# Two edits in a chunk-band attention layer: where background work may enter the VectorE queue, and which engine copies some of the queries

## The chip, the cores and the metric

The kernel runs on one core of one Trainium2 chip. The metric is the device time of one execution in microseconds (us), the median over several runs. The engines are named as in the profile: PE is TensorE's matmul unit and PEld its weight loads, DVE is VectorE, ACT is ScalarE, POOL is GpSimd, SP is SyncE, which here issues all DMAs.

## The reference, cut to what matters

Two layers of a streaming encoder are computed for a prompt of 2048 rows and a sample of 64 rows, each row 1024 wide. Layer A is a sliding-window attention with 16 heads and two key heads; layer B has 16 heads of its own keys and attends from each chunk of 64 rows to its own chunk and the eight before it.

```python
def gated_attention_layer(x_p, x_s, ck, cv, norm_g, w_in, q_g, k_g, w_out, ...):
    qp, kp, vp, gp = project(x_p, norm_g, w_in, q_g, k_g, n_heads, n_kv)
    op = prompt_band_attention(qp, kp, vp, past_chunks, bias_fn, sinks)
    y_p = x_p + (op * jax.nn.silu(gp)) @ w_out
    ...                                   # the same for the sample, with cached keys and values
def attend(q, k, v, bias, valid, sinks):
    s = jnp.einsum('bqkgd,bskd->bkgqs', qg, k).astype(jnp.float32) * (dh ** -0.5)
    s = s + bias.reshape(kv, g, tq, tk)
    ...
    p = jax.nn.softmax(s, axis=-1)        # layer B
```

`project` makes queries, keys, values and the gate with one matrix, and normalizes queries and keys per head.

## The kernel before, in words

**Precision by pairs.** Many operands are split in two numbers of fewer bits, a high part (ACT rounds it) and a low part (DVE takes the difference), and products are summed on PE over the parts. For the scores of layer B a head's high query `q1` stands twice in the 128 partitions, once in each half, and is multiplied with a key tile that holds the high keys in one half and the low keys in the other. So each query is needed in both halves. `q2` holds the low queries.

**The units.** The prompt is cut into eight units of 256 rows (0 to 7, each two tiles of 128), and the sample is unit 8 (`NU` is 8). The order in every pass is 0 to 6, the sample, then unit 7. Layer B makes eight passes, one for each pair of heads (`hp`). Each pass projects all nine units and attends in all nine; an entry of the list `its` is one unit of one pass.

**The order on PE** is written out by hand. `Filler` hands out the matmuls of the projections (L711 to L713) and of the output projections (L1858 to L1860) in small portions, and `pipeline` of layer B places the steps of attention between such portions. For each item it takes four steps (head and tile; the sample has one): `scores`, a share of background work, a portion of filler, then what is due from earlier steps (transposes of exponentials, products with the values). After the second step of a unit it calls `queries` for the next item; in the sample's only step it calls `queries` for unit 7 right after the sample's scores, and a portion of filler lies between that and unit 7's first scores.

**The order on the other engines** is made by a planner when the program is built, which places instructions by its own model of the times, within the dependencies. `Background` adds orderings to that: work put there (weight splits, norms, gates, low parts of queries) is released in portions by `bg.share`, and what is released is ordered behind the engine's "anchor", the last instruction given to `bg.anchor`. The ordering is no wait between engines.

**queries** (L1406) transposes the normalized queries and keys of an item into the one PSUM bank with the tag "tp"; ACT writes the high queries into one half of `q1` (L1431) and the high keys into half of `KA` or `KB` (L1432). For the sample the tiles are `QS`, `KSA` and `KSB`. `copies` then issues two DMAs that copy the high queries into the other half (L1436, shown as q<-q or QS<-QS); it is put into `held["later"]` and issued at the next `flush`. `low`, as urgent background work, makes the low queries (L1443) and low keys (L1447) on DVE. For the last two items of the whole layer (the sample and unit 7 of the last pass) `copies` isn't used, and `low` ends with an ACT copy instead (L1452). The last copy by DMA is kept in `held["copy"]`; the transposes by DMA of exponentials (L1553) are ordered behind it on SP's queue.

**scores** (L1459) computes one tile's scores into a bank with the tag "sb" (two buffers; L1492 and L1493, for the sample L1478). DVE adds the bias and takes the minimum of negated scores in one instruction (L1496; reading its accumulator is a second row of the profile). From the second pass on, except for the sample, DVE then adds a constant to the minimum (L1501, 128x1). ACT takes the exponential (L1505). The anchors are then the minimum `mi` on DVE and the exponential `ex` on ACT. After that `parts` makes the high part of the exponential on ACT (L1544) and the low part on POOL (L1545), and SP transposes both by DMA.

Other lines that will be named: L207 transposes two columns of maxima for the scales of the output weights, through the bank "tp"; L501 is the low part of a weight split; L807, L816 and L836 belong to the norms and the gate; L811 is POOL's power in the norm; L759 is ACT's evacuation of a projection's gate; L1650 is the product of transposed exponentials with the values.

## Time and profile before

| | |
|---|---|
| median of 3 runs | 2152.05 us |
| lowest, highest | 2145.67, 2154.64 us |
| the profiled execution | 2147.27 us, its span 2145.5 us |
| granted TensorE clock | 0.992 |
| busy: PE, DVE, ACT, POOL | 95%, 70%, 67%, 54% of the span |

The span goes from the first to the last instruction on the core. Layer B's attention runs from about 890 to 1990 us of it; one pass takes about 130 us. In the timeline an instruction's row has its start, its duration, engine, line, operation, output and inputs, and in brackets how long the engine stood idle before it and what ended that. A wait is put down to the releaser that came last by the profile.

### The profile page before, as it was taken

The numbers are of one execution on the slowest core, as the hardware profiler recorded it, in microseconds if no ns is written. First come the engines' busy times: TensorE is split into PE (matmuls) and PEld (weight loads), VectorE is DVE, ScalarE is ACT, GpSimd is POOL, SyncE is SP. The second block draws the span as 40 slices with busy tenths as digits, with TensorE's granted clock in tenths as the row PEclk, the third lists the DMA queues.
The fourth block names the chain that finished last, engine by engine and source line by source line (L and its number), as shares of the span: only waits on it lengthen the run. The fifth ranks groups of instructions, "written<-read, shape, count | busy, mean of one in ns | idle before, by whom it ended". The sixth has DMA issues, their size and how long they took to land.

```text
span 2145.5 us, 40906 instructions
## 1 busy us (share of the span) xinstructions
PE 2046.2 (95%) x12951; PEld 1467.4 (68%) x12951; DVE 1504.9 (70%) x4049; ACT 1428.7 (67%) x3610; POOL 1148.6 (54%) x1621
## 2 busy tenths in 40 slices
PE   7999999999999999888999999999999999898999
PEld 6887788778888999555555555555555555456887
DVE  6768778767767554677777777777867778577642
ACT  6878877767777333466667676777867768577420
POOL 5555544434445445774366676666766667566000
PEclk9999999999999999999999999999999999999999
DMA  8856545756544676744478799797887979668763
GB/s 277 269 168 209 176 155 191 211 168 212 163 149 133 211 220 182 243 149 156 136 173 205 186 194 224 169 229 177 194 213 175 241 156 202 153 144 193 228 198 116
DMA packets 512120, 404.96 MB, mean 189 GB/s; under 512 B 303696, under 2 KB 449376, under 8 KB 511872
## 3 DMA queue, kind: packets, MB, share of 16 engines
q1 hardware_dynamic: 511904, 402.35, 69.7%
q8 instruction: 102, 1.67, 0.3%
q14 instruction: 114, 0.93, 0.1%
HBM read 257.59 MB, written 73.43 MB: 154 GB/s over the span
## 4 chain that ended last, share of the span: by engine, by line
PE 62%; DVE 12%; ACT 8%; DMA 6%; issue 6%; POOL 4%; SPq 1%; ACTq 0%; DVEq 0%; POOLq 0%
PE pj L711 11%; PE pj L713 10%; PE pj L712 10%; PE pj L1858 4%; PE pj L1860 4%; PE pj L1859 4%; PE o L1650 3%; PE sa L900 2%; PE sb L1492 2%; PE tp L900 2%; PE sb L1493 2%; DVE p L1496 2%; DMA xraw<-in_x_rows_dram 1%; PE sa L1198 1%; DMA q<-q 1%
## 5 line engine op out<-in xcount | busy, mean ns | idle before, releaser
L711 PE MATMUL pj<-wh,xx 128*128 128x512 f16 (+2 forms) x1648 | 641.9, 389 | 5.3 <-ACT pb L734 2.9
L713 PE MATMUL pj<-wh,xx 128*128 128x512 f16 (+2 forms) x1648 | 623.9, 379 | 1.3 <-POOL xx L596 1.3
L712 PE MATMUL pj<-wh,xx 128*128 128x512 f16 x1024 | 390.1, 381 | 1.0 <-DVE wh L501 1.0
L1545 POOL TENSOR_TENSOR values<-p,values 128x640 f16<-128x640 f32 (+2 forms) x224 | 281.7, 1260 | 182.8 <-ACT values L1544 179.5
L1505 ACT ACTIVATE p<-p,nm 128x640 f32<-128x640 f32 (+5 forms) x264 | 199.6, 756 | 221.7 <-DVE nm L1501 175.1
L1858 PE MATMUL pj<-xx,wh 128*128 128x264 f32 (+1 forms) x1024 | 289.8, 283 | 5.8 <-DVE res L1868 3.1
L1859 PE MATMUL pj<-xx,wh 128*128 128x264 f32 (+1 forms) x1024 | 287.2, 280 | 0.0
L1496 DVE CUSTOM_DVE_ANT_0 p<-sb,BT 128x640 f32<-128x640 f32 (+5 forms) x272 | 196.5, 722 | 106.5 <-PE sb L1493 102.9
L712 PE MATMUL pj<-wl,xx 128*128 128x512 f32 (+1 forms) x624 | 233.8, 375 | 2.2 <-DVE wl L501 2.2
L596 POOL TENSOR_TENSOR xx<-xraw,xx 128x528 fp32r<-128x528 f32 (+4 forms) x144 | 185.4, 1307 | 89.3 <-ACT xx L595 75.9
L811 POOL TENSOR_TENSOR f<-f,mhalf 128x4 f32<-128x4 f32 (+2 forms) x187 | 191.5, 1025 | 11.4
L1312 POOL TENSOR_TENSOR o<-gt,o 128x256 f32<-128x256 f32 (+1 forms) x132 | 104.9, 795 | 152.7 <-ACT p L1215 91.7
L713 PEld LDWEIGHTS <-xx 128*128 128x128 f16 x1024 | 100.6, 98 | 125.4 <-issue 4.3
L816 DVE TENSOR_TENSOR pa<-pa,f 128x256 f32<-128x256 f32 (+3 forms) x221 | 143.9, 652 | 57.2 <-POOL f L811 52.4
L793 POOL TENSOR_TENSOR sq<-pa 128x256 f32<-128x256 f32 (+2 forms) x187 | 114.0, 610 | 120.1 <-ACT pa L747 79.2
L1215 ACT ACTIVATE p<-p,nm 128x257 f32<-128x257 f32 (+2 forms) x272 | 134.4, 497 | 50.5 <-DVE nm L1209 43.2
L711 PEld LDWEIGHTS <-xx 128*128 128x128 f16 x1024 | 100.9, 99 | 80.4 <-issue 2.2
L712 PEld LDWEIGHTS <-xx 128*128 128x128 f16 x1024 | 100.7, 98 | 80.1 <-issue 3.3
L1544 ACT CAST values<-p 128x640 f16<-128x640 f32 (+2 forms) x224 | 147.3, 658 | 8.3 <-DMA pt<-values 3.1
L1860 PE MATMUL pj<-xx,wl 128*128 128x264 f32 x512 | 145.4, 284 | 0.6 <-DVE wl L494 0.6
L1209 DVE CUSTOM_DVE_ANT_0 p<-sa,BT,nsink 128x256 f32<-128x256 f32 (+2 forms) x272 | 117.5, 468 | 38.3 <-PE sa L900 30.7
L1860 PE MATMUL pj<-xx,wh 128*128 128x264 f16 x512 | 141.3, 276 | 1.4 <-DVE wh L491 1.4
(279 smaller groups left out, 5023.4 us busy)
## 6 DMA issues: line engine op xcount, KB each, us to landing
xx<-xsb SPq DMA_DIRECT2D x112, 512.0 KB, 4.3
xx<-xsa SPq DMA_DIRECT2D x88, 512.0 KB, 4.9
xraw<-oga SPq DMA_DIRECT2D x64, 264.0 KB, 3.7
xraw<-ogb SPq DMA_DIRECT2D x64, 264.0 KB, 3.7
xsa<-xx SPq DMA_DIRECT2D x32, 512.0 KB, 4.0
wl<-in_w_in_b_dram SPq DMA_DIRECT2D x64, 256.0 KB, 5.1
wraw<-in_w_in_b_dram SPq DMA_DIRECT2D x56, 256.0 KB, 3.6
xraw<-in_x_dram SPq DMA_DIRECT2D x40, 256.0 KB, 3.9
```

The source lines that it names most:

```text
L596: nc.gpsimd.tensor_tensor(lo, rv, wide(hi), op=ALU.subtract)
L711: nc.tensor.matmul(ps[:n, :C], xh, wh, start=k == 0, stop=False)
L712: nc.tensor.matmul(ps[:n, :C], xh, wl, start=False, stop=False)
L713: nc.tensor.matmul(ps[:n, :C], xl, wh, start=False, stop=k == KC - 1)
L811: nc.gpsimd.tensor_tensor(fv, fv, mhalf[:n, :H], op=ALU.pow)
L1496: mi = nc.vector.tensor_tensor_reduce(out=p[r, :nk], in0=S[r, o : o + nk], in1=b, op0=ALU.add, op1=ALU.min, scale=1.0, scalar=3e38, accum_ ...
L1505: ex = nc.scalar.activation(p[:n, :nk], p[:n, :nk], AF.Exp, scale=-1.0, bias=it.nm[:n, c : c + 1], accum_out=it.sm[:n, c : c + 1],)
L1544: hi = nc.scalar.copy(two[:, :, 0, :], pv)
L1545: lo = nc.gpsimd.tensor_tensor(two[:, :, 1, :], pv, two[:, :, 0, :], op=ALU.subtract)
L1858: nc.tensor.matmul(ps[:, :OT], wh, oh, start=k == 0, stop=False)
L1859: nc.tensor.matmul(ps[:, :OT], wh, ol, start=False, stop=False)
L1860: nc.tensor.matmul(ps[:, :OT], wl, oh, start=False, stop=k == KC - 1)
```

## The change: an anchor behind the addition, and copies of queries by ScalarE

In `scores` the name `mi` is given to the addition (L1501) where there is one, so that `bg.anchor(mi, ex)` orders background work on DVE behind the addition and not only behind the minimum. In `queries` a test `direct` picks the sample and unit 7 of every pass (`it.unit[0] >= NU - 1`; the last two items are among them). For these ACT writes the high queries into the other half itself, in `queries`, straight from PSUM and next to the other activations; `copies` isn't put into `held["later"]`, so `held["copy"]` stays what it was. The ACT copy at the end of `low` is gone.

```diff
+        def direct(it):
+            return it.unit[0] >= NU - 1 or it in its[-2:]
+
         def queries(it):
...
             for hh, rows in enumerate(halves):
                 nc.scalar.activation(q1[hh][rows], qt[hh], AF.Identity, scale=gq[rows])
                 nc.scalar.activation(kd[hh][rows], kt[hh], AF.Identity, scale=gk[rows])
+                if direct(it):
+                    nc.scalar.activation(q1[hh][halves[1 - hh]], qt[hh], AF.Identity, scale=gq[rows])
 
             def copies():
                 for hh, rows in enumerate(halves):
                     held["copy"] = load(wide(q1[hh][halves[1 - hh]]), wide(q1[hh][rows])).ins
 
-            if it not in its[-2:]:
+            if not direct(it):
                 held["later"].append(copies)
 
             def low(hh, rows):
...
-                    if it in its[-2:]:
-                        nc.scalar.activation(
-                            q1[hh][halves[1 - hh]], qt[hh], AF.Identity, scale=gq[rows]
-                        )
                 return fn
...
             if turned(it, h):
-                nc.vector.tensor_scalar(
+                mi = nc.vector.tensor_scalar(
                     it.nm[:, c : c + 1], it.nm[:, c : c + 1], math.log(PB), 1.0,
                     op0=ALU.add, op1=ALU.mult,
                 )
```

## The prediction, made before the changed kernel was run

> **What bounds the kernel now.** I read the page first: its engine totals, the chain that ended last, and the costliest groups.

> ```profile
> span 2145.5 us, 40906 instructions
> PE 2046.2 (95%) x12951; PEld 1467.4 (68%) x12951; DVE 1504.9 (70%) x4049; ACT 1428.7 (67%) x3610; POOL 1148.6 (54%) x1621
> ...
> L1505 ACT ACTIVATE p<-p,nm 128x640 f32<-128x640 f32 (+5 forms) x264 | 199.6, 756 | 221.7 <-DVE nm L1501 175.1
> ```

> TensorE (PE) is busy for 95% of the span; VectorE (DVE) and ScalarE (ACT) for about 70%. So a microsecond is won only where PE stands still. The last row shows what edit one is about: ACT, ahead of the exponentials of layer B, stood idle for 175.1 us until the addition at L1501 had run. That is large, but it is ACT's idle time, not PE's. So I asked next for the waits of PE alone, in the stretch of layer B (1020 to 1975 us). Columns: who waited for whom, us in total, times, longest.

> ```profile
> PE sb L1492 <- DVE nm L1496: 11.5, 8, 1.9
> PE tp L207 <- DVE KB L1447: 6.9, 1, 6.9
> PE sb L1492 <- DMA q<-q: 6.1, 4, 1.9
> PE sb L1478 <- DMA QS<-QS: 4.8, 3, 1.8
> ...
> PE sb L1492 <- ACT q L1452: 1.5, 1, 1.5
> ...
> PE sb L1478 <- DVE nm L1501: 1.1, 1, 1.1
> ...
> PE sb L1492 <- ACT pb L759: 1.0, 1, 1.0
> ```

> No exponential appears as a releaser: PE doesn't wait for one directly. What the change can reach is the copies of the queries, q<-q and QS<-QS, 10.9 us. The last two rows belong to them as well, as will be seen; L1452 is in the pair of items where ACT makes the copy already.

> The timeline of one head pair shows the place; the other pairs repeat it. Columns: start, duration, engine and line, and in brackets the engine's idle time before it with its releaser. First all engines:

> ```profile
> 1296.07 0.28 DVE L1443 SCALAR_TENSOR_TENSOR QS<-tp,qsc,QS 64x64 fp32r<-64x64 f32 x1 [1.30 <-ACT KSB L1432]
> ...
> 1297.00 1.40 SPq L1436 DMA_DIRECT2D QS<-QS  x2
> ...
> 1300.99 0.83 ACT L1505 ACTIVATE p<-p,nm 128x640 f32<-128x640 f32 x1 [1.57 <-DVE nm L1501]
> ...
> 1301.17 0.53 PE L1478 MATMUL sb<-KSA,QS 128*128 128x320 f32 x2 [1.30 <-DMA QS<-QS]
> ...
> 1301.94 0.72 ACT L1544 CAST values<-p 128x640 f16<-128x640 f32 x1
> ...
> 1305.25 0.45 ACT L1431 ACTIVATE q<-tp,qf 64x256 f16<-64x256 f32 x1
> ...
> 1306.46 0.46 ACT L1432 ACTIVATE KB<-tp,kf 64x256 f16<-64x256 f32 x1
> ...
> 1306.80 1.13 SPq L1436 DMA_DIRECT2D q<-q  x2
> ...
> 1306.95 0.47 DVE L1443 SCALAR_TENSOR_TENSOR q<-tp,qf,q 64x256 f16<-64x256 f32 x1 [0.75 <-ACT KB L1432]
> ...
> 1307.46 0.48 DVE L1447 SCALAR_TENSOR_TENSOR KA<-tp,kf,KA 64x256 f16<-64x256 f32 x1
> ...
> 1310.62 0.32 PE L1492 MATMUL sb<-KA,q 128*128 128x384 f16 x1 [1.71 <-DMA q<-q]
> ```

> Then DVE alone, around the sample's scores:

> ```profile
> 1298.63 0.81 DVE L1496 CUSTOM_DVE_ANT_0 p<-sb,BT 128x640 f32<-128x640 f32 x1
> 1299.37 0.08 DVE L1496 DVE_READ_ACCUMULATOR2_ANT nm<- 128x1 f32 x1
> 1299.37 0.41 DVE L807 TENSOR_REDUCE f<-sq 128x4 f32<-128x256 f32 x1
> 1299.70 1.13 DVE L836 SCALAR_TENSOR_TENSOR pb<-sq,pb 128x128 f32<-128x128 f32 x1
> 1300.75 0.14 DVE L1501 TENSOR_SCALAR nm<-nm 128x1 f32<-128x1 f32 x1
> 1302.01 0.42 DVE L816 TENSOR_TENSOR pa<-pa,f 128x256 f32<-128x256 f32 x1 [1.11 <-POOL f L811]
> 1302.35 0.48 DVE L1496 CUSTOM_DVE_ANT_0 p<-sb,BT 64x320 f32<-64x320 f32 x1
> ```

> PE reaches the sample's scores (L1478) at 1301.17 - 1.30 = 1299.87 and is held by the copy of QS. It reaches the first score of unit 7, which follows, at 1310.62 - 1.71 = 1308.91, with everything ready but the copy of q. Two stalls in a pass, 3.0 us.

> **Edit two, the copies by ACT: what goes.** By the order of units, "sample or unit 7" are two of nine items of each head pair. Seven pairs lose two DMAs in each; the eighth makes its copies on ACT already, and there they move ahead of the low parts. The stalls that the copies own: at unit 7, 6.1 us and the 1.0 put down to L759 (an evacuation that only stands last in the record; the stall has the place and size of its sisters), together 7.1 in five passes; at the sample, 4.8 and the 1.1 put down to L1501 (the same reason), together 5.9 in four.

> **What comes.** The added instruction exists in the trace, in the last pair:

> ```profile
> L1452 ACT ACTIVATE QS<-tp,qsc x2: 307/309/311, 1960.7 to 1962.2; 64x64 fp32r<-64x64 f32 x2
> L1452 ACT ACTIVATE q<-tp,qf x2: 467/469/471, 1970.7 to 1972.2; 64x256 f16<-64x256 f32 x2
> ```

> 14 x 0.31 + 14 x 0.47 = 10.9 us of ACT, which is idle a third of the time. They aren't free, though: DVE's low parts (L1443, L1447) began at 1306.95, when the last of the four activations (1306.46 + 0.46) had ended, though the first was done at 1305.70; at the sample the row of 1296.07 says the same, behind KSB. I take it that they will wait for all six. Four activations took 1305.25 to 1306.92, 0.42 each; two more put the low parts of unit 7 back by 0.84. PE needs the first pair of low parts only, as another pass shows, where PE started while the second L1443 was running:

> ```profile
> 1179.42 0.49 DVE L1443 SCALAR_TENSOR_TENSOR q<-tp,qf,q 64x256 f16<-64x256 f32 x1
> ...
> 1179.50 0.32 PE L1492 MATMUL sb<-KA,q 128*128 128x384 f16 x1 [0.95 <-DMA q<-q]
> ```

> So what is late next at unit 7 is L1447 of KA: 1307.46 + 0.48 + 0.84 = 1308.78, just under PE's arrival at 1308.91, and the stall would be gone. But PE will arrive earlier, by what the sample's stall gave back (1.3), while ACT's queries hang on the sample's minima (1302.35), and these stand behind L816, which waited for GpSimd and not for PE. If these stay where they are, 1.2 us of each stall returns. Between 0 and 1.2 I take 0.5: with S ready earlier the minima may well be placed ahead of L816. Unit 7 gives 7.1 - 5 x 0.5 = 4.6.

> At the sample the next late thing is the bank of scores, free when the minimum of 1298.63 ends (1299.37 + 0.08 = 1299.45), or up to 0.6 later if the two small activations push DVE's low parts and with them that minimum: at most 1300.07, against 1299.87. I take 0.1 each: 5.9 - 0.4 = 5.5.

> In the last pair L1492 waited for the first L1452, 1.5 us; the low parts, pushed by the copies now ahead of them, take its place. I keep 0.4 of it.

> One cost stands against this. The second-longest row of the waits, L207, is a transpose for which the one bank "tp" must be free of unit 7's queries, between pairs 6 and 7:

> ```profile
> 1830.28 0.49 DVE L1447 SCALAR_TENSOR_TENSOR KB<-tp,kf,KB 64x256 f16<-64x256 f32 x1
> ...
> 1830.92 0.58 PE L207 MATMUL tp<-ident,top 128*1 128x128 f32 x2 [6.88 <-DVE KB L1447]
> ```

> There all four low parts count, and 0.84 more is paid in full: +0.8.

> The transposes by DMA (L1553) on SP's queue are ordered behind the last copy; that copy is now unit 6's, so around the sample they may go out earlier, and 28 issues fewer stand before them. Nobody waits for their result: their reader L1650 idled 0.9 us in all, for something else.

> ```profile
> L1650 PE MATMUL o<-pt,values 128*128 128x256 f16 (+1 forms) x1176 | 125.7, 255 | 0.9 <-ACT o L1622 0.9
> ```

> So that is 0.

> [...]

> **Edit one, the anchor on the addition.** The same DVE work in another order: L836 (1.13 us above) behind L1501, not ahead. The exponential of 1300.99 could start at 1299.7. The cost on DVE is nothing, since the addition runs anyway; work moved behind it is 0.14 later. What it gains is ACT's time, and PE waits for ACT hardly anywhere. The longest row of PE's waits, 11.5 us for minima at L1496, has its regular place at unit 6:

> ```profile
> 1280.03 1.30 DVE L501 SCALAR_TENSOR_TENSOR wh<-wl,gsb,wh 128x512 f16<-128x512 f32 x1
> ...
> 1281.56 0.48 DVE L1443 SCALAR_TENSOR_TENSOR q<-tp,qf,q 64x256 f16<-64x256 f32 x1
> ...
> 1283.77 0.81 DVE L1496 CUSTOM_DVE_ANT_0 p<-sb,BT 128x640 f32<-128x640 f32 x1
> ...
> 1284.65 0.32 PE L1492 MATMUL sb<-KA,q 128*128 128x384 f16 x1 [1.36 <-DVE nm L1496]
> ```

> DVE has there 1.30 us of L501, then the low parts of the next unit's queries, four of 0.48 or so by their rows at unit 7, and only then the minimum that PE waits for; the addition's place among them changes nothing in their sum. So I take 0, between -11.5 (all of that row) and the loss of the third rival.

> **Sum.** -4.6 - 5.5 - 0.4 + 0.8 = -9.7, say -10. The profiled execution took 2147.27 us (span 2145.5), 4.8 under the median of the runs, 2152.05, whose spread is 9; so 2137 for an execution like the profiled one and 2142 for the median. About 0.5% (10.7 us) is what a measurement of this kernel can tell from no change, so the forecast lies on that edge.

> **Rivals.**
> *More is won (0.15).* Earlier exponentials bring the casts, GpSimd's work and the evacuations forward, DVE gets through unit 6 earlier, and some of the 11.5 us goes too, besides all of unit 7. For it: ACT's 175.1 us of idling. Against: DVE full at that place. At most 7.1 + 5.9 + 1.5 + 11.5 = 26; with half of the 11.5 it is 20, less the 0.8: 2133.
> *The wait only changes its name (0.18).* Unit 7 keeps 1.2 in each of five passes (7.1 - 6.0 = 1.1 won), the sample waits 0.2 in each of four (5.1 won): 1.1 + 5.1 - 0.8 = 5.4, 2147. For it: L816 waiting for GpSimd, and low parts that begin only behind the whole batch. Against: the sample's scores come earlier.
> *Slower (0.14).* On ACT an exponential that is ready earlier gets a place ahead of the next unit's queries (L1431). With the cast behind it that is 0.83 + 0.72 = 1.55 us, by which low parts, the next minimum and the bank come later; where DVE is full, as at unit 6, PE pays it all. It decides from seven such places on (10 / 1.55); at two of nine units in each of seven passes it costs 14 x 1.55 = 21.7: 2142 + 21.7 = 2164. For it: the order on ACT is made anew by a planner. Against: the queries are asked for before the scores whose exponential would pass them, and most units have slack, since PE's wait for minima has only 8 entries.

> **How the numbers follow.** The forecast has 0.53, within 2138 to 2147 (the stalls of unit 7 gone wholly and the sample's as well, 7.1 + 5.9 + 1.5 = 14.5 less 0.8; or the second rival's 5.4 as its other end). The range goes from 2127 (the first rival nearly whole) to 2155 (the second, with the spread of the runs, and the mild part of the third). Faster by over 0.5%: the first rival and under half of the forecast, 0.15 + 0.25 = 0.40. Slower by over 0.5%: most of the third, 0.12. The rest, 0.48, is within.

> **What would show it.** Right: no QS<-QS among PE's waits, and no q<-q at unit 7; L1478 with under 0.3 us of idle time; at unit 7 a rest of 0 to 1.2 with DVE (KA, L1447) as the releaser; L207 near 7.7; ACT's wait for L1501 well under 175, with PE's wait for L1496 still near 11. Wrong: L1492 waiting for L1496 in more than 15 places, or the stall at unit 6 gone.

## The result, and the profile after

Six executions of each kernel: 2163.87 us after (2160.74 to 2166.85) against 2148.55 before, a ratio of 1.0068 [1.0048, 1.0088]. The change costs 0.7%; the forecast was 0.5% less, with 2155 as its upper end. The profiled execution took 2165.26 us, its span was 2163.4, its mean granted TensorE clock 0.986 (before 0.992).

The page after:

```profile
PE 2060.8 (95%) x12951; PEld 1472.0 (68%) x12951; DVE 1515.9 (70%) x4049; ACT 1441.9 (67%) x3638; POOL 1140.8 (53%) x1621
```

PE runs the same 12951 matmuls and is busy 14.6 us longer. From here on lines of `queries` and `scores` are numbered as in the changed kernel: the minimum is L1497, the addition L1502, the exponential L1506, the copy by ACT L1437, the low queries and keys L1448 and L1452, POOL's low part L1546, the sample's product on POOL L1616. PE's waits of layer B (1020 to 1990 us):

```profile
PE sb L1493 <- DVE nm L1497: 14.7, 7, 2.7
PE o L900 <- POOL o L1616: 11.6, 6, 3.0
PE tp L207 <- DVE KB L1452: 5.6, 1, 5.6
PE pj L711 <- DVE values L754: 4.8, 5, 1.0
PE o L1651 <- DVE o L1311: 3.8, 7, 0.9
PE sb L1493 <- DVE f L807: 2.6, 1, 2.6
```

The waits for the copies (QS<-QS, and q<-q but for 0.5 us) are gone, as the second edit means them to be. In their place stand three others: the second row was 3.2 us before and is now 11.6; the fourth and the fifth were under 1 us each. The first has grown by 3.2, and the 2.6 us put down to L807 are one more stall at its regular place, unit 6.

Where the time goes is read by passes. I took the five passes between the sample's scores of the second pair and of the seventh. These are the last lines of two tables by windows, before first, then after; the first number is the length:

```profile
sum 650.70, PE 627.08 PEld 360.59 DVE 489.96 ACT 480.46 POOL 439.11; mean PE 125.42 PEld 72.12 DVE 97.99 ACT 96.09 POOL 87.82
```

```profile
sum 672.00, PE 638.84 PEld 363.99 DVE 505.12 ACT 491.00 POOL 436.37; mean PE 127.77 PEld 72.80 DVE 101.02 ACT 98.20 POOL 87.27
```

The five passes are 21.3 us longer: PE stands still 33.2 us instead of 23.6 (+9.5), and is busy 11.8 us longer with the same work. (The span grew by less, 17.9, because the changed kernel came to the first of these passes 3.8 us earlier.) Two stalls come back in every pass: in these five, PE's stalls at unit 6 come to 13.3 us instead of 6.7, and those behind the sample to 11.3 instead of 3.3. One is at unit 6, where VectorE's order has changed. DVE before and then after, start and duration first:

```profile
1409.07 0.82 DVE L1496 CUSTOM_DVE_ANT_0 p<-sb,BT 128x640 f32<-128x640 f32 x1
...
1409.81 0.68 DVE L175 TENSOR_REDUCE most<-wraw 128x1 f32<-128x512 f32 x1
1410.41 1.30 DVE L501 SCALAR_TENSOR_TENSOR wh<-wl,gsb,wh 128x512 f16<-128x512 f32 x1
...
1411.76 0.14 DVE L1501 TENSOR_SCALAR nm<-nm 128x1 f32<-128x1 f32 x1
...
1414.16 0.81 DVE L1496 CUSTOM_DVE_ANT_0 p<-sb,BT 128x640 f32<-128x640 f32 x1
```

```profile
1415.93 0.82 DVE L1497 CUSTOM_DVE_ANT_0 p<-sb,BT 128x640 f32<-128x640 f32 x1
...
1417.15 1.42 DVE L501 SCALAR_TENSOR_TENSOR wh<-wl,gsb,wh 128x512 f16<-128x512 f32 x1 [0.40 <-ACT wh L498]
1418.49 0.14 DVE L1502 TENSOR_SCALAR nm<-nm 128x1 f32<-128x1 f32 x1
1418.56 0.67 DVE L175 TENSOR_REDUCE most<-wraw 128x1 f32<-128x512 f32 x1
...
1419.28 0.47 DVE L1448 SCALAR_TENSOR_TENSOR q<-tp,qf,q 64x256 f16<-64x256 f32 x1
...
1421.49 0.81 DVE L1497 CUSTOM_DVE_ANT_0 p<-sb,BT 128x640 f32<-128x640 f32 x1
```

Before, the maximum L175 (0.68) ran in the time between the minimum and the weight split L501. Now L175 may only come behind the addition, L501 still stands ahead of it, and DVE idles 0.40 us for ACT. But ACT isn't what holds L501 longest. POOL has a low part in work there, before and then after:

```profile
1409.76 1.40 POOL L1545 TENSOR_TENSOR values<-p,values 128x640 f16<-128x640 f32 x1
```

```profile
1416.62 1.40 POOL L1546 TENSOR_TENSOR values<-p,values 128x640 f16<-128x640 f32 x1
1424.52 0.73 DVE L501 SCALAR_TENSOR_TENSOR wh<-wl,gsb,wh 128x512 f16<-128x512 f32 x1
```

L501 takes 0.73 us in its shortest rows, in which no low part runs beside it (last row). Here it takes 1.30 and 1.42, and both times it ends 0.55 us behind the low part and 2.64 us behind the start of the minimum. So in either order DVE came past L501 only behind POOL's low part. L175 used to lie in that time, and now it comes on top. In three of the other four passes the idle time is only 0.12 us and L501 takes 1.70 instead, and the sum is the same: from minimum to minimum DVE needs 5.56 us instead of 5.09.

That is 0.47 of the 1.30 us by which the stall grows here. The rest is a later beginning: PE reaches the bank 4.59 us after the first of these minima started before the change, and 3.77 us after it now. PE's side of it before:

```profile
1415.03 0.32 PE L1492 MATMUL sb<-KA,q 128*128 128x384 f16 x1 [1.37 <-DVE nm L1496]
```

And after:

```profile
1419.32 0.38 PE L713 MATMUL pj<-wh,xx 128*128 128x512 f16 x1
1422.37 0.32 PE L1493 MATMUL sb<-KA,q 128*128 128x384 f16 x1 [2.67 <-DVE nm L1497]
...
1423.32 0.63 PE L712 MATMUL pj<-wh,xx 128*128 128x512 f16 x1
1423.75 0.63 PE L713 MATMUL pj<-wh,xx 128*128 128x512 f16 x1
...
1426.31 0.39 PE L713 MATMUL pj<-wh,xx 128*128 128x512 f16 x1
```

Behind the stall the matmuls of 512 columns start 0.43 us apart, eight times, until they fall back to 0.21: the stall has cost the clock as well, about 1.7 us more. In a row of a table by windows the third number from the end is the granted clock, here 0.50:

```profile
1422.90:1426.31 3.41, 3.41 (x11) 1.20 (x9) 3.30 (x7) 2.76 (x8) 2.31 (x3) 0.50 0.96 289
```

The trace's records of the granted clock have seven such stretches of 3.41 us in the five passes, five at the stalls of unit 6 and two behind the sample's, and none before the change. Half of 7 x 3.41 is 11.9 us: that is PE's longer busy time.

The other stall is behind the sample, on POOL's queue. Before, then after:

```profile
1459.52 0.32 POOL L1615 TENSOR_TENSOR o<-G,o 128x64 f32<-128x64 f32 x1 [0.98 <-DVE o L1614]
...
1461.33 1.40 POOL L1545 TENSOR_TENSOR values<-p,values 128x640 f16<-128x640 f32 x1
```

```profile
1465.12 0.46 DVE L1615 TENSOR_TENSOR o<-tp,o 64x64 f32<-64x64 f32 x2
1466.49 0.14 POOL L348 MEMSET BT<- 64x64 f32 x1 [1.75 <-DMA BT<-skew]
1466.59 1.39 POOL L1546 TENSOR_TENSOR values<-p,values 128x640 f16<-128x640 f32 x1
1467.94 0.31 POOL L1616 TENSOR_TENSOR o<-G,o 128x64 f32<-128x64 f32 x1
```

The low part of an exponential, 1.4 us long, now stands ahead of the sample's small product. PE's transpose L900 waits for that product: 1.93 us in this pass, up to 2.96 in others, against at most 0.7 before.

The low part isn't all of it. The product's operands were ready at 1465.58, when L1615 ended. Until 1466.49 POOL stood still: ahead of the low part, a fill of the bias tile (L348) waited for the load of that tile. Before the change the fill stood ahead of the product too, but its load was there in time. On SP's queue that load went out between two transposes of exponentials, and now it goes out behind both, before and then after:

```profile
1455.42 0.33 SPq L347 DMA_DIRECT2D BT<-skew  x1
1456.62 1.27 SPq L1553 DMA_TRANSPOSE pt<-values  x1
```

```profile
1459.03 4.53 SPq L1554 DMA_TRANSPOSE pt<-values  x2
1463.66 0.62 SPq L347 DMA_DIRECT2D BT<-skew  x1
```

So of the 2.36 us by which the product is late, 0.91 are the load's and 1.45 those of the fill and the low part. In each of the five passes the fill waits like this, 1.75 to 2.25 us in all.

### The profile page after: what moved, and what is told of

The parts are those of the page before. It is cut to its first block, busy times and chain, and to the rows that moved or that the text cites. A ratio compares the mean times of both kernels' runs of the same rounds, so it can differ in the third digit from the quotient of the medians.

```text
span 2163.4 us, 40853 instructions
## 1 busy us (share of the span) xinstructions
PE 2060.8 (95%) x12951; PEld 1472.0 (68%) x12951; DVE 1515.9 (70%) x4049; ACT 1441.9 (67%) x3638; POOL 1140.8 (53%) x1621
## 4 chain that ended last, share of the span: by engine, by line
PE 62%; DVE 12%; ACT 8%; issue 6%; DMA 6%; POOL 5%; SPq 1%; ACTq 0%; POOLq 0%; DVEq 0%
PE pj L711 11%; PE pj L712 11%; PE pj L713 11%; PE pj L1859 4%; PE pj L1861 4%; PE pj L1860 4%; PE o L1651 3%; PE sa L900 2%; DVE p L1497 2%; PE tp L900 2%; DVE wh L501 2%; PE sb L1493 2%; PE sb L1494 2%; PE sa L1198 1%; POOL f L811 1%
## 5 line engine op out<-in xcount | busy, mean ns | idle before, releaser
L1546 POOL TENSOR_TENSOR values<-p,values 128x640 f16<-128x640 f32 (+2 forms) x224 | 282.2, 1260 | 144.8 <-ACT values L1545 133.3
L1506 ACT ACTIVATE p<-p,nm 128x640 f32<-128x640 f32 (+5 forms) x264 | 199.5, 756 | 219.0 <-DVE nm L1502 165.4
L1497 DVE CUSTOM_DVE_ANT_0 p<-sb,BT 128x640 f32<-128x640 f32 (+5 forms) x272 | 196.6, 723 | 122.7 <-PE sb L1494 119.4
L811 POOL TENSOR_TENSOR f<-f,mhalf 128x4 f32<-128x4 f32 (+2 forms) x187 | 188.8, 1011 | 11.6
L816 DVE TENSOR_TENSOR pa<-pa,f 128x256 f32<-128x256 f32 (+3 forms) x221 | 146.8, 666 | 60.3 <-POOL f L811 56.8
L712 PEld LDWEIGHTS <-xx 128*128 128x128 f16 x1024 | 101.6, 99 | 86.8 <-issue 11.2
```

The source lines that it names most:

```text
L712: nc.tensor.matmul(ps[:n, :C], xh, wl, start=False, stop=False)
L811: nc.gpsimd.tensor_tensor(fv, fv, mhalf[:n, :H], op=ALU.pow)
L1497: mi = nc.vector.tensor_tensor_reduce(out=p[r, :nk], in0=S[r, o : o + nk], in1=b, op0=ALU.add, op1=ALU.min, scale=1.0, scalar=3e38, accum_ ...
L1506: ex = nc.scalar.activation(p[:n, :nk], p[:n, :nk], AF.Exp, scale=-1.0, bias=it.nm[:n, c : c + 1], accum_out=it.sm[:n, c : c + 1],)
L1546: lo = nc.gpsimd.tensor_tensor(two[:, :, 1, :], pv, two[:, :, 0, :], op=ALU.subtract)
```

## The experiments

Ratios are to the kernel before, run on the same chip beside them, with the 95% interval.

### Which of the two edits?

`anchor_only` takes the first edit alone (its lines are numbered as before the change), `copies_only` the second; `copies_sample` and `copies_unit7` take the second for one of its two items:

```diff
# copies_sample                                  # copies_unit7
-            return it.unit[0] >= NU - 1 or it in its[-2:]
+            return it.unit[0] == NU or it in its[-2:]      # or: == NU - 1
```

> Edit one alone: the anchor on the addition; all copies of queries stay as before. Theory H (the changed kernel is late because PE, relieved of the copies, runs into work of DVE, ACT and POOL that it cannot hurry, and its clock falls behind the longer stalls): the copies still hold PE, so nothing much changes: ratio 0.998 to 1.002, the stall at unit 6 stays 1.2 to 1.6 us, clock 0.992. Rival O (the new order of background work is itself the loss: weight splits behind the addition lengthen DVE's way to the minimum that frees the bank): ratio 1.005 to 1.010, the stall at unit 6 grows to 2 us or more and the clock falls to 0.988 or lower.

> Edit two alone: ACT copies the queries of the sample and of unit 7 in every pass; the anchor stays on the minimum. Theory H: the stalls at the sample and at unit 7 are gone, the one at unit 6 grows to over 2 us with the clock falling behind it, ratio 1.003 to 1.008. Rival O: the stalls go and little comes in their place, ratio 0.993 to 0.997.

> Half of edit two: ACT copies the queries of the sample only; unit 7 of every pass but the last keeps its copy by DMA; the anchor stays on the minimum. Theory H: the stall of the sample (1.3 to 1.8 us in four passes) moves to unit 7, where the copy's issue hangs on ACT and not on PE: 1.7 becomes 2.5 to 3; ratio 0.999 to 1.003. Rival O: 5 us won, ratio 0.997.

> The other half of edit two: ACT copies the queries of unit 7 only; the sample keeps its copy by DMA; the anchor stays on the minimum. Theory H: the stall of unit 7 (1.0 to 1.9 us in five passes) goes, and half of it or more comes back at unit 6 of the next pass; ratio 0.998 to 1.004. Rival O: 6 us won, ratio 0.997.

Measured: `anchor_only` 1.0116 [1.0101, 1.0131], `copies_only` 0.9972 [0.996, 0.9985], `copies_sample` 1.0017 [1.0004, 1.0031], `copies_unit7` 0.9992 [0.9978, 1.0006]. My first theory, that the copies take the cover from PE and run it into the other engines' chain, falls: the copies win 6.0 us. The order of the background work loses 25 us by itself, and has both stalls; the one behind the sample has grown more:

```profile
PE sb L1492 <- DVE nm L1496: 16.2, 8, 2.7
PE o L900 <- POOL o L1615: 13.9, 6, 3.5
```

In `copies_only` PE waits 4.9 us for the evacuation L754 and 4.6 for the low query L1448, both at unit 7. In `copies_sample`:

```profile
PE sb L1493 <- DMA q<-q: 18.4, 7, 3.7
```

With the copy by ACT at the sample alone, the stall saved there comes back at unit 7, whose DMA copy PE now awaits for 18.4 us instead of 6.1. The two copies only pay together.

### Which operation is in the wrong place?

Four variants of the whole change. `scan_behind_min` puts L175 back behind the minimum, `product_on_dve` takes the sample's product off POOL's queue, past the fill and the low part, `both_back` does both, and `stall_filled` fills the stall behind the sample with matmuls:

```diff
# scan_behind_min: bg.first holds the minimum, bg.anchors the addition
-            if r.ins.engine in bg.anchors:
-                behind(r.ins, bg.anchors[r.ins.engine])
+            if r.ins.engine in bg.first:
+                behind(r.ins, bg.first[r.ins.engine])
# product_on_dve
-            nc.gpsimd.tensor_tensor(o, it.G[:, 0:HD], o, op=ALU.mult)
+            nc.vector.tensor_tensor(o, it.G[:, 0:HD], o, op=ALU.mult)
# stall_filled
             tp = o_bank()
+            for _ in range(6):
+                nc.tensor.matmul(tp[:, 0:512], held["VH"][:, 0, 0], KA[:, 0:512], start=True, stop=True)
             transpose(tp[0:HD, 0:P], it.o)
```

> The changed kernel with one thing put back: the maximum over a weight tile (L175) is again ordered behind the minimum, not behind the addition; all other background work stays behind the addition. Theory M (two places carry the loss: at unit 6 VectorE idles 0.40 us ahead of the low part L501 because L175 no longer fills that gap, which makes PE's stall 1.4 -> 2.7 us and lowers the clock behind it; at the sample GpSimd takes the next low part ahead of the sample's product, 0.65 -> 2.3 us): the stall at unit 6 goes back to at most 1.7 us a pass, the slow matmuls behind it (near 1287, 1423, 1557, 1691, 1824) go, and the time falls by about 8 us to a ratio near 1.003. The stalls for L1616 stay (total near 11) unless the later exponential moves them too. Rival P (DVE's chain is full: whichever work is placed where, the stall only moves): the sum of PE's waits for DVE stays within 2 us of that of the changed kernel and the ratio stays 1.005 to 1.009.

> The changed kernel with the sample's product (L1616, 128x64) on VectorE instead of GpSimd, so that no low part and no fill of the bias tile stands ahead of it. Theory M: PE's wait for L1616 (11.6 us in six places) falls below 2 us, the slow matmuls behind those of over 2.2 us go, and the time falls by about 10 us, to a ratio of 1.000 to 1.003; the stall at unit 6 stays at 14.7 us in all. Rival P: the wait returns as one for VectorE in the same place (over 1 us each), ratio 1.005 to 1.009.

> Both of these in the changed kernel: L175 behind the minimum, the sample's product on VectorE. Theory M: both losses go, the clock is back at 0.991 or more, and the time is near that of the copies alone or a little better: ratio 0.993 to 0.999. Rival P: above 1.003.

> The changed kernel with six matmuls of 512 columns (1.3 us at full clock) into the sample's free bank ahead of the transpose that waits for L1616; what they write is written over. They lie in time in which PE idles where the stall is over 1.3 us, and keep it from idling long. If the long stalls themselves lower the clock behind them (theory C): no slow matmuls behind the sample's stalls (near 1199, 1335, 1962), so 1 to 2 us less behind each of three, against up to 1 us more where the stall is shorter: ratio 1.003 to 1.007, clock up by 0.001 to 0.002. If the clock is lowered by something else (rival D): the slow matmuls stay, the clock as in the changed kernel (0.986), and the time is the same or up to 4 us longer, ratio 1.006 to 1.010.

Measured: 1.0034 [1.0017, 1.0051], 1.0025 [1.001, 1.004], 1.0046 [1.0027, 1.0065] and 1.0085 [1.0064, 1.0107]. Each of the first two gives back about half, as theory M has it, but the two don't add. PE's waits say why; `scan_behind_min`, `product_on_dve`, `both_back`:

```profile
PE o L1651 <- DVE o L1311: 7.9, 8, 1.2
...
PE o L900 <- POOL o L1616: 0.3, 1, 0.3
```

```profile
PE sb L1493 <- DVE nm L1497: 16.2, 8, 2.7
```

```profile
PE o L1651 <- DVE o L1311: 7.9, 8, 1.2
...
PE o L900 <- DVE nm L1502: 3.4, 4, 0.8
```

With L175 behind the minimum DVE needs 4.97 us from minimum to minimum at unit 6, and the stall there is 1.6 us in three of the five passes. In the planner's new order POOL's low part and the fill stand behind the sample's product again: 11.6 us become 0.3. So nothing is left for the second repair to win; it adds a wait for DVE of 3.4 us. In place of the two stalls a third has grown, for the sums of outputs L1311, which are ordered behind the addition as well.

In `stall_filled` no slow matmuls follow the stalls behind the sample (in the changed kernel they do after the two of 2.25 and 2.96 us in these passes), but the six matmuls take 1.3 us of PE each time, and the time doesn't fall. By its time this run decides nothing between C and D; that the stretches of 0.50 behind the sample's stalls are gone speaks for C, and so do the counts at the end.

### Work that meets POOL's low part

In the groups of DVE's instructions (1170 to 1820 us) three kinds have a longer mean after the change, L816, L836 (473 to 512 ns) and L501 (1159 to 1218 ns). With L175 back L816 is at 840. L816 before, then after:

```profile
L816 DVE TENSOR_TENSOR pa<-pa,f 128x256 f32<-128x256 f32 (+1 forms) x85 | 59.4, 700 | 28.0 <-POOL f L811 27.0
```

```profile
L816 DVE TENSOR_TENSOR pa<-pa,f 128x256 f32<-128x256 f32 (+1 forms) x83 | 62.1, 753 | 32.6 <-POOL f L811 32.6
```

The mean hides two durations. Of the changed kernel:

```profile
1373.46 0.41 DVE L816 TENSOR_TENSOR pa<-pa,f 128x256 f32<-128x256 f32 x1
```

```profile
1367.48 1.39 POOL L1546 TENSOR_TENSOR values<-p,values 128x640 f16<-128x640 f32 x1
1367.55 1.60 DVE L816 TENSOR_TENSOR pa<-pa,f 128x256 f32<-128x256 f32 x1
```

Alone it takes 0.41 us. Begun 0.07 us after a low part on POOL it takes 1.60 and ends 0.28 after it. The rows of L501 above are of the same kind. I read the longer rows as standing until POOL is done; the traces show when they end, not why. The maximum L175 isn't touched: 0.65 to 0.69 us in all its 107 rows of this stretch in the two traces, also in the 18 that meet a low part of 1.4 us. The addition is what the exponential, the cast and then the low part wait for, so work ordered behind it comes nearer to the low part.

`norms_behind_min` puts L816 and L836 back behind the minimum, `norms_scan_min` L175 as well; `norms_on_pool` runs L816 on POOL, where it can't meet the low part, and `copies_norms_pool` does that without the first edit:

```diff
# norms_behind_min, norms_scan_min (it.fnname: the name of the piece of background work)
-                a = self.anchors.get(x.engine)
+                a = (self.first if it.fnname in ("scale", "product") else self.anchors).get(x.engine)
# norms_on_pool, copies_norms_pool
-            nc.vector.tensor_tensor(sv, sv, fv.unsqueeze(2).to_broadcast([n, H, HD]), op=ALU.mult)
+            (nc.gpsimd if apart else nc.vector).tensor_tensor(sv, sv, fv.unsqueeze(2).to_broadcast([n, H, HD]), op=ALU.mult)
```

> The changed kernel with only VectorE's head scale (L816) and gate product (L836) put back behind the minimum; the maximum over a weight tile (L175) and the rest stay behind the addition. These two read two SBUF operands and take 0.3 to 0.5 us alone, but up to 1.6 us where GpSimd's low part (L1546) runs: over the passes they cost VectorE 44 us above their short form before, 53 in the changed kernel, 66 with L175 behind the minimum. Theory L (the addition is where GpSimd's low part follows, so work behind it meets that low part, and this lengthens VectorE's way): their excess falls to 46 or less, VectorE's busy time of the six passes falls by 5 us or more, and the time falls to a ratio of 1.001 to 1.004; the stall at unit 6 loses only what the shorter way gives. Rival W (those are stretched in time that VectorE has to spare; only the place of L175 and of the sample's product counts): the ratio stays 1.005 to 1.009.

> The changed kernel with L816, L836 and L175 behind the minimum, so that only the low parts, L501, L754, L1311 and the reciprocal are still ordered behind the addition. Theory L: all three costs of the order are gone, PE's busy time of six passes falls from 766 (L175 alone back) to 757 or less, and the time is that of the copies alone: ratio 0.995 to 0.999. Rival W: no better than with L175 alone back, ratio 1.002 to 1.005.

> The changed kernel with the head scale (L816, layer B) on GpSimd instead of VectorE. It can then meet no low part, since GpSimd runs both in turn. Theory L: VectorE loses 60 us of busy time over the passes, PE's stall at unit 6 falls below 2 us, and the time falls by 8 us or more, ratio below 1.003, unless GpSimd's queue (52% busy, some 10 us more a pass) makes low parts late: then PE's waits for the transposed tiles (L1651) grow instead. Rival W: the time stays within 1.005 to 1.009 with the stall at unit 6 at 2.6 us.

> The copies alone (work behind the minimum as before) with the head scale (L816, layer B) on GpSimd. If VectorE's meetings with GpSimd's low part cost time even in this order (24 us of stretch over the passes in L816), the stalls at unit 6 (1.4 us) and at unit 7 (0.8 and 1.0 us) shrink and the time falls below the copies alone: ratio 0.990 to 0.996. If GpSimd's queue makes low parts late, 1.000 or more.

Measured: 1.004 [1.0026, 1.0054], 1.0065 [1.0043, 1.0087], 1.0011 [0.9999, 1.0023], 0.9972 [0.9957, 0.9986]. L816 on POOL takes 0.57% off the changed kernel and nothing off the copies alone (0.9972 both times). So its time on DVE is dear in the new order and free in the old one. How much of that is the meeting with the low part, and how much simply a shorter way for DVE, these runs don't separate: in `norms_behind_min` L816 has the lowest mean of all (584 ns), and 0.4% is lost all the same. `norms_scan_min` was a miss for both theories: three kinds of work back in their old place, and hardly better than the change. There L1311 holds PE for 7.0 us and the sample's product for 5.6; why the planner's order comes out so stays open.

### Which places of a pass?

Kind by kind the cost doesn't add up. The last runs cut by unit: the changed kernel, with the addition as the anchor in some units only and the minimum in the others. `pool_both` joins the two repairs by another engine.

```diff
-            bg.anchor(mi, ex)
+            bg.anchor(mi if u in (6,) else least, ex)      # (0,), (1, 2, 3, 4, 5, 7), (5, 7), (0, 1, 2, 3, 4, 6)
```

> The changed kernel (ScalarE's copies and all), but with the background work behind the addition only while unit 6 is scored; in all other units it stands behind the minimum. Theory S (the loss sits at two seams of a pass: at unit 6, and at unit 0 behind the sample; the other units have time to spare): PE's stall at unit 6 is 2.3 to 2.7 us a pass, the stall for the sample's product stays below 1 us, ratio 1.000 to 1.004 (copies alone 0.9972). Rival V (the loss is spread over all units, by work that comes later everywhere): ratio 0.997 to 1.000, the stall below 2 us.

> The changed kernel with the background work behind the addition only in unit 0. Theory S: the wait for the sample's product is 1.9 us or more a pass, the stall at unit 6 is 1.4 us as with the copies alone, ratio 0.999 to 1.003. Rival V: that wait stays below 1 us, ratio 0.996 to 0.999.

> The changed kernel with the background work behind the addition in units 1 to 5 and 7, and behind the minimum in units 0 and 6 and the sample. Theory S: neither stall grows (unit 6 below 1.8 us, the sample's product below 1 us), ratio 0.996 to 1.000. Rival V: ratio 1.002 to 1.006.

> The changed kernel with the head scale (L816, layer B) on GpSimd, which took it from 1.0068 to 1.0011, and the sample's product (L1616) on VectorE, which is what PE still waits for there (10.1 us in six places). If the two costs lie on different stalls they add: the wait for L1616 goes, ratio 0.995 to 0.998, level with the copies alone. If the stall only moves on: 1.000 to 1.003.

Measured: `anchor_u6` 0.9989 [0.9978, 0.9999], `anchor_u0` 0.9978 [0.9965, 0.9991], `anchor_rest` 1.0077 [1.0059, 1.0094], `pool_both` 0.996 [0.9945, 0.9975]. The first three are the reverse of theory S, and `anchor_rest` has both stalls in full (16.2 and 11.2 us): I had named the units at which PE waits, not those whose order makes it wait. The work that delays unit 6's scores, the low parts of its queries and L175, stands among unit 5's last pairs; the low part ahead of the sample's product is that of unit 7's last pair. So one more cut:

> The changed kernel with the background work behind the addition only in units 5 and 7. The run before showed both stalls with units 0 and 6 left out, so the places were misnamed: the work that stands ahead of unit 6's scores is put behind unit 5's last additions, and the low part that stands ahead of the sample's product belongs to unit 7's last pair. Theory S, with these units: both stalls are back (2.66 us at unit 6 and 1.8 us or more for L1616, a pass), ratio 1.004 to 1.009. Rival V (spread over all units): ratio 0.999 to 1.003.

> The changed kernel with the background work behind the addition in all units but 5 and 7. Theory S: neither stall grows (1.4 us at unit 6, below 1 us for L1616), ratio 0.996 to 1.000, as with the copies alone. Rival V: ratio 1.003 to 1.006.

Measured: 1.0039 [1.0023, 1.0056] and 1.0001 [0.9985, 1.0017]. PE's waits for the sample's product, with units 5 and 7, then with all the others:

```profile
PE o L900 <- POOL o L1616: 10.0, 6, 2.2
```

```profile
PE o L900 <- POOL o L1616: 3.2, 5, 0.6
```

The stall behind the sample comes with units 5 and 7: 10.0 us with them and 3.2 without. By its place it is unit 7's, but no run separates the two. The stall at unit 6 has both sources: 1.37 us a pass with the copies alone, mostly 1.85 and 1.78 here, 2.67 with all. With units 5 and 7 DVE's way is the long one (5.56) but begins as before, 4.59 us ahead of PE; only with units 1 to 4 as well (`anchor_rest`) does it begin at 3.77. Which of their work makes it late stays open. Against the copies alone (0.9972) units 5 and 7 cost 0.67% and the others 0.29%, together the 0.96% by which the whole change stands above them. So by the medians of these runs, each good to about 0.15%, two thirds sit at two units and one third is spread.

`pool_both` is the best of all: the change as it was made, with L816 on POOL and the sample's product on DVE, 8 us below the kernel before. From `norms_on_pool` the product gives 0.5%, as it gave 0.43% from the change, so these two repairs add. It isn't told apart from the copies alone by its interval, so nothing here shows a gain from the first edit, only that its cost can be taken away.

## Why the prediction was wrong

**Edit one, the step that failed.** The prediction took it as zero, by "the addition's place among them changes nothing in their sum", and counted 1.30 us of L501 as work. The sum isn't fixed. L501's shortest rows take 0.73; beside POOL's low part it ended 0.55 us behind that in all 33 rows of the two traces, and L175 had lain in the time before. (L836's 1.13 us in the prediction is such a row too: it takes 0.28 alone.) Behind the addition it comes on top: 5.56 us from minimum to minimum instead of 5.09. The same holds for all of DVE: 4049 instructions before and after, and 11 us more of busy time. And the order reaches other queues: on POOL's, a fill that waits for its load and a low part of 1.4 us now stand ahead of a product that PE awaits. Why DVE also begins 0.82 us later at unit 6 is known by units only. "PE waits for ACT hardly anywhere" was right and beside the point. Alone the edit costs 25 us.

**The bounds of that step.** Its upper bound was the third rival, 22 us, a price of the right size with the wrong mechanism, so that it came near is luck: at unit 6 the low queries L1448 follow in DVE's row without idle time for ACT, so no exponential holds back the queries. The check "L1492 waiting for L1496 in more than 15 places" didn't see it, since the places went from 8 to 7 and most grew.

**What no term stood for** is the clock: 11.8 of the 21.3 us in five passes are slower matmuls at and behind longer stalls (seven stretches of 3.41 us at a granted clock of 0.50).

**The copies, term by term.** The mechanism was right, the size too large: -9.7 foreseen, -6.0 measured alone (0.9972). At the sample the stall went, as forecast. At unit 7 the term of -4.6 came to nothing: 7.2 us of stalls over 0.6 us in five passes became 8.7, for a stall of 1.7 became 0.80 for the low query and 0.97 for the evacuation L754, `copies_only`:

```profile
1308.03 0.48 DVE L1448 SCALAR_TENSOR_TENSOR q<-tp,qf,q 64x256 f16<-64x256 f32 x1 [1.71 <-ACT q L1437]
```

```profile
1307.43 0.33 PE L1493 MATMUL sb<-KA,q 128*128 128x384 f16 x1
1308.56 0.34 PE L1494 MATMUL sb<-KA,q 128*128 128x384 f16 x1 [0.80 <-DVE q L1448]
...
1310.42 0.38 PE L711 MATMUL pj<-wh,xx 128*128 128x512 f16 x1 [0.97 <-DVE values L754]
```

PE's first product now starts unhindered at 1307.43, but the low parts wait for all six activations (1.71 us of idle DVE), as was taken, and hold up the second product; that the four low parts also push L754, and with it PE's next bank, was not looked at. The terms were also added as if independent; at the sample alone the copy wins nothing (1.0017). L207 came out at 7.7 with the copies alone, as forecast (+0.8), and at 5.6 in the whole change.

**The rest of the checks.** No QS<-QS: right. ACT's wait for the addition "well under 175": 165.4, so even what the edit was to win moved little. L1478, now L1479, was to idle under 0.3 us; it idled about 0.5 us twice.

## What to carry to other kernels

An ordering constraint without a wait is still a schedule: before it is costed at zero, list for each engine what now comes earlier and what that passes in the next queue, for here the loss was on GpSimd and the edit on VectorE. An operation that fills another's wait is lost to it once it may only come later, though the sum of the work stays the same. Look for the clock behind a stall that has grown, too: here, with PE busy 95% of the time, 3.41 us at a granted clock of 0.50 followed a stall of 2.67 us and cost 1.7 us on top of it. And a row's busy time can be more than its work, as for L816, 0.41 us alone and 1.60 beside a low part: before it is counted as work, look for the shortest row of the same line.

## What the runs showed of the hardware

Rows of L501 and L816 on VectorE that met POOL's low part of 1.4 us mostly ended a fixed time behind it. In 18 of 18 such meetings before the change and 15 of 15 after it, between 1170 and 1820 us, L501 ended 0.55 us behind the low part; L816 ended 0.28 us behind it in 17 of 35 and in 28 of 35, and over 1.2 us before the low part's end in 13 and in 5.
